# A two-request encoder layer on one core: a lead between the two streams of each merged stage

## The chip, the cores and the metric

The kernel runs on one core of a Trainium2 chip. The metric is device time in microseconds (us) for one launch, in which both request groups pass through the whole layer. Three runs of the kernel before gave 2291.81, 2293.14 and 2294.97 us; the median is 2293.14.

The engines are called as the profile calls them: PE is the matrix engine (PEld its weight loads), ACT the scalar engine, DVE the vector engine, POOL the general one, and SP the engine that issues most of the DMA transfers. Each takes its instructions in a fixed order: an instruction that waits holds back all behind it on the same engine.

## What is computed

One layer is applied to two sequences that share the weights: the prompt (stream 0, 1024 tokens) and the sample (stream 1, 512 tokens), each with 16 meta tokens in front. Cut to what matters:

```
n = rms_norm(h, g_mix);  qa,ka,va,qb,kb,vb = split(n @ w_in)
A: 8 query heads on 2 key heads, softmax(q k^T / 8) v     (q, k normalised and rotated)
B: 4 heads, (softmax(q0 k0^T/8) - lam * softmax(q1 k1^T/8)) v, then a norm
h = h + concat(A, B) @ w_out
n = rms_norm(h, g_ffn)
h = h + (gelu(conv3(n @ w_gate)) * (n @ w_up)) @ w_down        (ConvGLU, 22 column tiles of 128)
out = rms_norm(h, g_final)
```

## The kernel before

Every dense product is done as three passes in a reduced float format (`mm3`, lines 129 to 131: high part by high part, high by low, low by high), so activations and weights are split into a high part (a cast on ACT, line 123) and a low part (a subtraction on DVE or POOL, line 124). `dense` makes one output tile of 128 features by up to 512 tokens from 8 k-tiles, which is 24 matmuls.

For each stream there are four pieces, written as Python generators that yield an estimate of the matmul columns they have just issued:

- `projection`: w_in. Its keys tile comes first; the head norm of a tile is a matmul too (line 232), and waits for squares from ACT and POOL. Queries and keys go to DRAM (`qk`, line 247).
- `attention`: loads q and k with line 370 on SP, makes scores into the PSUM tile `ps_s` (lines 401 and 402), scales them on DVE (line 405), exponentiates on ACT (408), transposes on PE (422), splits into `pt_hi` and `pt_lo`, and multiplies by v into `ps_o` (432 to 437, 446; for heads B line 541 adds the norm). Results go to DRAM (`oT`, lines 482 and 563), and the reciprocals of heads A make a round trip through DRAM (`rT`, lines 458 and 474).
- `mixer_out`: reads `oT` back into `h` (line 612, SP), splits it into `xhi` and `xlo`, multiplies by w_out and adds the input.
- `conv_glu`: the feed-forward part, in 11 groups of two column tiles.

The program runs these stages: the sample's projection alone; stage 1, the sample's attention merged with the prompt's projection; stage 2, the prompt's attention merged with the sample's mixer and ConvGLU; the prompt's mixer; the prompt's ConvGLU alone. `ps_s` is one buffer in both merged stages, and `ps_o` is one too.

What sets the order: `merge` takes the next step of whichever generator is behind by its weighted count (`done[0]/wa` against `done[1]/wb`), and so gives the order in which instructions are traced. A planner then fixes each engine's own order. Of what its model of the timeline has ready it takes, by and large, what was traced first, so that an instruction traced later can still come earlier on its engine. `issue_after(x)` tells it that the instructions traced in a block stand behind x on x's engine, and on that engine alone. In the kernel before, `merge` is never given its last argument, so that nothing is held. At the end of stage 2 the program opens six PSUM buffers and merges the prompt's mixer with what is left of the sample's ConvGLU (line 884).

Of the kernel before, what the change touches and what calls it, by code (L numbers as in the profile page):

```python
# [20 lines left out]
P = 128  # L21
D = 1024
KT = D // P
# [103 lines left out]
def mm3(g, ps, whi, wlo, xhi, xlo, start, stop):  # L127
    nc = g.nc
    nc.tensor.matmul(ps, lhsT=whi, rhs=xhi, start=start, stop=False)  # L129
    nc.tensor.matmul(ps, lhsT=whi, rhs=xlo, start=False, stop=False)  # L130
    nc.tensor.matmul(ps, lhsT=wlo, rhs=xhi, start=False, stop=stop)  # L131


def dense(g, ps, w, xhi, xlo, c0, cw, order=range(KT)):

    whi, wlo = w
    for i, k in enumerate(order):
        mm3(g, ps, whi[:, k * P:(k + 1) * P], wlo[:, k * P:(k + 1) * P],
            xhi[k][:, c0:c0 + cw], xlo[k][:, c0:c0 + cw], i == 0, i == KT - 1)


def load_weight(g, src, lo_engine=None, hi_engine=None):
# [206 lines left out]
def attention(ctx, g, s, side):  # L349
    nc, tc = g.nc, g.tc  # L350
# [43 lines left out]
    def softmax(q, k, l):  # L394

        M = q[0].shape[-1]
        p = pp.tile([P, ne], F32, name="p", tag="p")[:M]
        ps = g.psum.wide(M, nch, kw)
        for i in range(nch):
            kc = k[:, i * kw:(i + 1) * kw]  # L400
            nc.tensor.matmul(ps[:, i], lhsT=q[0], rhs=kc, start=True, stop=False)  # L401
            g.mark = nc.tensor.matmul(ps[:, i], lhsT=q[1], rhs=kc, start=False, stop=True).ins  # L402

        nm = sp.tile([P, 1], F32, name="nm", tag="nm")[:M]
        nc.vector.tensor_scalar(out=p.rearrange("p (i w) -> p i w", i=nch), in0=ps, scalar1=-HD ** -0.5, scalar2=3.0e38,  # L405
                                op0=ALU.mult, op1=ALU.min, accum_out=nm)
        p = p[:, :n]
        nc.scalar.activation(p, p, AF.Exp, bias=nm, scale=-1.0, accum_out=l)  # L408
        return p

    def weighted_v(pl, v, diff):

        W = sum(p.shape[0] for p in pl)
        o = g.psum.tile(P, W, "o")
        v, v_tail = v

        def transposed(k0, kw):
            tps = g.psum.tile(kw, W, "t")
            c = 0
            for p in pl:  # L420
                M = p.shape[0]
                nc.tensor.transpose(tps[:, c:c + M], p[:, k0:k0 + kw], g.ident[:M, :M])  # L422
                c += M
            return tps

        for i in range(nf):
            tps = transposed(i * P, P)
            hi = ptp.tile([P, 512], F32R, name="pt_hi", tag="pt_hi")[:, :W]
            lo = ptp.tile([P, 512], F32R, name="pt_lo", tag="pt_lo")[:, :W]
            split(g, hi, lo, tps)  # L430
            if diff:
                nc.tensor.matmul(o, lhsT=v[:, i, 0:P], rhs=hi, start=i == 0, stop=False)  # L432
                nc.tensor.matmul(o, lhsT=v[:, i, P:2 * P], rhs=hi, start=False, stop=False)  # L433
                nc.tensor.matmul(o, lhsT=v[:, i, 0:P], rhs=lo, start=False, stop=False)  # L434
            else:
                nc.tensor.matmul(o, lhsT=v[:, i, :], rhs=hi, start=i == 0, stop=False)  # L436
                nc.tensor.matmul(o, lhsT=v[:, i, :], rhs=lo, start=False, stop=False)  # L437
            yield 5 * W

        tps = transposed(n - 32, 32)  # L440
        parts = ptp.tile([P, 512], F32R, name="pt_hi", tag="pt_hi")[:, :W]
        split(g, parts[0:32], parts[32:64], tps)
        if diff:
            nc.scalar.copy(parts[64:96], tps)
        rows = v_tail.shape[0]
        nc.tensor.matmul(o, lhsT=v_tail, rhs=parts[:rows], start=False, stop=True)
        yield 2 * W
        return o, W

# [35 lines left out]
    for kv in range(2):  # L485
        k = load_k(KA, kv)
        v = load_v(0, P, kv * P)
        for i in range(4):
            h = kv * 4 + i
            for b in range(nblk):  # L490
                q = load_q(QA + 2 * kv, i, NMETA + 512 * b, 512)
# [8 lines left out]
                o, W = yield from weighted_v(pl, v, False)  # L500
# [13 lines left out]
        o, W = yield from weighted_v([p], v, False)  # L514
# [37 lines left out]
    for h in range(4):  # L552
        ks = [load_k(KB + h // 2 * 2, h % 2 * 2 + m) for m in range(2)]
        v = load_v(1 + h, 2 * P, 0)
        rows = g.oT[s][512 + h * P:512 + (h + 1) * P]
        for blk in blocks:
            c0 = blk[0][0]
# [3 lines left out]
            lead = 1 if c0 < NMETA else 0  # L561
# [22 lines left out]
def mixer_out(g, s, st, side, whole, tag):  # L584

    nc, tc = g.nc, g.tc
    C = SEQS[s] + 2
    h, rstd = st.h, st.rstd
    chunks = token_chunks(s)
    cm = max(w for _, w in chunks)  # L590
    with ExitStack() as es:
        mp = pool(es, g, f"fm{s}", 3, side)
        waiting = []

        def finish():
            while waiting:
                c0, cw, acc = waiting.pop(0)
                mean_rsqrt(g, mp, rstd[:, c0:c0 + cw], acc, cw, tag)

        for group in ([chunks] if whole else [[c] for c in chunks]):  # L600
            if whole:
                (xhi, xlo), base = [[x[:, k] for k in range(KT)] for x in st.x], 0
            else:
                xhi = [mp.tile([P, cm], F32R, name="xhi", tag=f"xhi{k}", bufs=2) for k in range(KT)]
                xlo = [mp.tile([P, cm], F32R, name="xlo", tag=f"xlo{k}", bufs=2) for k in range(KT)]
                base = group[0][0]
            acc = mp.tile([P, sum(w for _, w in group)], F32, name="acc", tag="acc", bufs=1 if whole else 2)
            if group[0][0] == 0:

                nc.vector.memset(h[:, :, C - 1:], 0.0)  # L610
                for k in range(KT):
                    nc.sync.dma_start(out=h[:, k, :C - 1], in_=g.oT[s][k * P:(k + 1) * P])
# [139 lines left out]
        yield 4 * cw  # L752


def merge(a, wa, b, wb, g=None):


    done = [0.0, 0.0]
    while True:
        i = 0 if b is None or done[0] / wa <= done[1] / wb else 1  # L760
        try:
            with g.tc.issue_after(g.mark) if g and i and g.mark else nullcontext():
                done[i] += next((a, b)[i])
# [12 lines left out]
PADD = 8  # L776
ML = 2
NRAW, NW = 2, 3
R1, R2, R3 = (1.0, 1.1), (1.0, 1.1), (1.0, 1.0)


@with_exitstack
def trunk_kernel(ctx, tc, g):
    nc = tc.nc
# [80 lines left out]
    with ExitStack() as es0:  # L865
        p0 = projection(es0, g, 0, "left", "mm", "mm")
        with ExitStack() as es1:
            merge(attention(es1, g, 1, "right"), R1[0], p0, R1[1])
        drain(p0)
    g.psum.close()  # L870
    g.psum = Psum(tc, "psb", mm=2)
# [1 line left out]
    with ExitStack() as es1:  # L873
        st1 = state(es1, 1, "right", True)

        def sample():
            yield from mixer_out(g, 1, st1, "right", True, "mm")
            yield from conv_glu(es1, g, 1, st1, "right", 1)
        f1 = sample()
        with ExitStack() as es0:  # L880
            merge(attention(es0, g, 0, "left"), R2[0], f1, R2[1])
        g.psum.relay(s=6)
        st0 = state(ctx, 0, "left", False)
        merge(mixer_out(g, 0, st0, "left", False, "s"), R3[0], f1, R3[1])
        drain(f1)
    xp = pool(ctx, g, "fx0", 1, "right")
    st0.x = [xp.tile([P, KT, SEQS[0] + 2], F32R, name=nm) for nm in ("xhi", "xlo")]
    g.psum.close()
# [66 lines left out]
```

## Time and profile before

The profiled execution took 2291.51 us; its span from the first instruction to the last is 2289.6 us. The busy times below are those of a window's engines; the clock is the mean granted to PE, as a share of full speed.

| stretch (us) | what runs | PE busy | ACT busy | clock |
|---|---|---|---|---|
| 0 to 157.5 | sample's projection | | | |
| 157.5 to 505.4 | stage 1, up to the last projection tile | 325.0 of 347.9 | 185.6 | 0.97 |
| 505.4 to 585.7 | sample's attention alone, then a stop | 39.7 of 80.3 | 37.6 | 0.78, 0.59 |
| 585.7 to 1323.3 | stage 2, up to the last sample tile but two | 730.9 of 737.6 | 442.4 | 1.00 in the main part |
| 1323.3 to 1402.3 | prompt's attention alone | 57.7 of 79.0 | 56.3 | 0.82, 0.81 |
| 1402.3 to 1540 | prompt's mixer | 122.6 of 137.7 | 73.9 | 0.91 |
| 1540 to 2289.6 | prompt's ConvGLU | | | |

How to read it: where PE is busy for the whole of a stretch at clock 1.00, the stretch lasts as long as its matmuls. Where it isn't, something else ends last, and matmuls that run there cost more than their own time.

### The profile page before, as it was taken

To read this page: it belongs to the slowest core of one execution; us is meant where nothing else is said; L and a number is where in the kernel's file an instruction comes from. 1 tells how busy PE (TensorE), PEld (TensorE's weight loads), DVE (VectorE), ACT (ScalarE), POOL (GpSimd) and SP (SyncE) were. 2 spreads that over 40 slices of the span, in tenths; PEclk is the share of its full clock that TensorE was granted. 3 is DMA by queue.
4 is the path that set the end of the run, shared out by engine and by line. 5 is a ranking of instruction groups with operands and counts; after the bars stand their busy time and mean duration, and the time that the engine had idled before them with its cause. 6 is when DMAs were issued, how large, how long until landed. Compare 5 with 4: busy or idle time off the path is not lost.

```text
span 2289.6 us, 32358 instructions
## 1 busy us (share of the span) xinstructions
PE 2143.9 (94%) x12442; PEld 1918.7 (84%) x12442; DVE 1287.9 (56%) x2203; ACT 1039.3 (45%) x1830; POOL 662.4 (29%) x514
## 2 busy tenths in 40 slices
PE   6888999986799999999999977989999999999997
PEld 6887999885788888888898966988888888888886
DVE  6636564454476667677777764764333444433446
ACT  5434555555454445557777785542122211122224
POOL 4862455440132211224343432431110001111004
PEclk9999999997899999999999987999999999999999
DMA  6563444443412332223333303631111111111112
GB/s 201 180 219 118 150 151 132 157 160 102 149 61 74 93 98 75 81 78 104 102 101 99 104 25 127 199 108 56 37 56 47 46 47 46 42 51 56 46 38 74
DMA packets 114259, 222.76 MB, mean 97 GB/s; under 512 B 16312, under 2 KB 67384, under 8 KB 113592
## 3 DMA queue, kind: packets, MB, share of 16 engines
q1 hardware_dynamic: 85304, 115.82, 15.7%
q10 hardware_dynamic: 28800, 104.87, 14.6%
q8 instruction: 98, 1.61, 0.3%
q14 instruction: 57, 0.47, 0.1%
HBM read 172.10 MB, written 48.55 MB: 96 GB/s over the span
## 4 chain that ended last, share of the span: by engine, by line
PE 66%; DVE 5%; ACT 3%; DMA 2%; issue 1%; POOL 1%; SPq 0%; DVEq 0%; ACTq 0%
PE ps_mm L129 17%; PE ps_mm L130 17%; PE ps_mm L131 17%; PE ps_t L422 4%; PE ps_s L401 3%; PE ps_s L402 2%; PE ps_o L437 1%; PE ps_o L436 1%; DVE p L405 1%; PE ps_o L432 1%; PE ps_o L434 1%; DVE y L729 1%; PE ps_o L433 1%; DVE w_lo L124 1%; DMA w_f<-w_out 1%
## 5 line engine op out<-in xcount | busy, mean ns | idle before, releaser
L129 PE MATMUL ps_mm<-xhi,w_hi 128*128 128x512 f32 (+6 forms) x1968 | 664.7, 338 | 26.2 <-ACT xhi L123 25.5
L130 PE MATMUL ps_mm<-xlo,w_hi 128*128 128x512 f32 (+6 forms) x1968 | 658.8, 335 | 0.0
L131 PE MATMUL ps_mm<-xhi,w_lo 128*128 128x512 f32 (+6 forms) x1968 | 658.8, 335 | 0.0
L129 PEld LDWEIGHTS ps_mm<-xhi,w_hi 128*128 128x128 f32 x1968 | 373.5, 190 | 52.6 <-ACT xhi L123 26.1
L130 PEld LDWEIGHTS ps_mm<-xlo,w_hi 128*128 128x128 f32 x1968 | 373.1, 190 | 25.1 <-issue 0.5
L131 PEld LDWEIGHTS ps_mm<-xhi,w_lo 128*128 128x128 f32 x1968 | 373.1, 190 | 24.7 <-issue 0.6
L123 ACT CAST w_hi<-w_f 128x1024 fp32r<-128x1024 f32 x134 | 139.3, 1048 | 399.2 <-PE ps_mm L130 361.8
L405 DVE TENSOR_SCALAR_CACHE_REDUCE p<-ps_s 114x1044 f32<-114x1044 f32 (+5 forms) x212 | 223.4, 1054 | 129.9 <-PE ps_s L402 103.1
L124 POOL TENSOR_TENSOR a_lo<-gate,a_hi 128x512 fp32r<-128x512 f32 x66 | 98.9, 1498 | 662.7 <-ACT a_hi L123 656.8
L123 ACT CAST pt_hi<-ps_t 128x512 fp32r<-128x512 f32 (+6 forms) x360 | 170.0, 483 | 208.8 <-PE ps_t L422 189.1
L408 ACT ACTIVATE p<-p,nm 114x1040 f32<-114x1040 f32 (+5 forms) x212 | 215.3, 1015 | 90.7 <-DVE p L405 89.9
L703 DVE TENSOR_TENSOR h<-ps_mm,h 128x512 f32<-128x512 f32 (+1 forms) x288 | 182.5, 645 | 129.4 <-PE ps_mm L131 128.2
L124 DVE TENSOR_TENSOR pt_lo<-ps_t,pt_hi 128x512 fp32r<-128x512 f32 (+4 forms) x312 | 172.2, 563 | 107.0 <-ACT pt_hi L123 105.6
L401 PE MATMUL ps_s<-k,q 128*114 128x348 f32 (+4 forms) x552 | 183.8, 338 | 38.5 <-DVE p L405 21.3
L131 PE MATMUL ps_mm<-a_hi,w_lo 128*128 128x512 f32 (+1 forms) x576 | 215.5, 377 | 0.6 <-DVE w_lo L151 0.6
L130 PE MATMUL ps_mm<-a_lo,w_hi 128*128 128x512 f32 (+1 forms) x576 | 215.6, 377 | 0.0
L129 PE MATMUL ps_mm<-a_hi,w_hi 128*128 128x512 f32 (+1 forms) x576 | 214.2, 384 | 0.0
L422 PE MATMUL ps_t<-ident,p 128*128 128x128 f32 (+7 forms) x1188 | 185.6, 272 | 2.4 <-DVE pt_lo L124 2.4
L402 PE MATMUL ps_s<-k,q 128*114 128x348 f32 (+4 forms) x552 | 176.0, 324 | 6.2 <-DMA q<-qk 6.2
L422 PEld LDWEIGHTS ps_t<-ident,p 128*128 128x128 f32 (+7 forms) x1188 | 143.9, 137 | 32.7 <-issue 8.4
L124 DVE TENSOR_TENSOR w_lo<-w_f,w_hi 128x1024 fp32r<-128x1024 f32 x100 | 122.7, 1236 | 83.4 <-ACT w_hi L123 83.2
L691 DVE TENSOR_TENSOR gate<-ps_mm,gate 128x512 f32<-128x512 f32 x66 | 45.6, 690 | 200.2 <-PE ps_mm L131 197.7
(189 smaller groups left out, 3627.6 us busy)
## 6 DMA issues: line engine op xcount, KB each, us to landing
w_f<-w_gate ACTq DMA_DIRECT2D x44, 512.0 KB
w_f<-w_up ACTq DMA_DIRECT2D x44, 512.0 KB
w_f<-w_down ACTq DMA_DIRECT2D x44, 512.0 KB
w_f<-w_in ACTq DMA_DIRECT2D x36, 512.0 KB
w_f<-w_out ACTq DMA_DIRECT2D x32, 512.0 KB
q<-qk SPq DMA_DIRECT2D x48, 256.0 KB
q<-qk SPq DMA_DIRECT2D x48, 171.0 KB
qk<-hi SPq DMA_DIRECT2D x20, 384.0 KB
```

The source lines that it names most:

```text
L123: nc.scalar.copy(hi, src)
L124: (lo_engine or nc.vector).tensor_tensor(out=lo, in0=src, in1=hi.bitcast(F32), op=ALU.subtract)
L129: nc.tensor.matmul(ps, lhsT=whi, rhs=xhi, start=start, stop=False)
L130: nc.tensor.matmul(ps, lhsT=whi, rhs=xlo, start=False, stop=False)
L131: nc.tensor.matmul(ps, lhsT=wlo, rhs=xhi, start=False, stop=stop)
L401: nc.tensor.matmul(ps[:, i], lhsT=q[0], rhs=kc, start=True, stop=False)
L402: g.mark = nc.tensor.matmul(ps[:, i], lhsT=q[1], rhs=kc, start=False, stop=True).ins
L405: nc.vector.tensor_scalar(out=p.rearrange("p (i w) -> p i w", i=nch), in0=ps, scalar1=-HD ** -0.5, scalar2=3.0e38, op0=ALU.mult, op1=ALU.m ...
L408: nc.scalar.activation(p, p, AF.Exp, bias=nm, scale=-1.0, accum_out=l)
L422: nc.tensor.transpose(tps[:, c:c + M], p[:, k0:k0 + kw], g.ident[:M, :M])
L691: nc.vector.tensor_tensor(out=a, in0=up, in1=a, op=ALU.mult)
L703: nc.vector.tensor_tensor(out=hs, in0=ps, in1=hs, op=ALU.add)
```

## The change

`merge` gets a lead and a hold. The count of the second generator starts at `lead` instead of zero: a negative lead lets the second generator run ahead, a positive one the first. The first `hold` steps of the stream that stays behind are traced inside `issue_after(mark)`, where `mark` is the last matmul that the leading stream had traced when the first of them came: on PE they can't be planned ahead of it. `mark` is now the last matmul of a dense tile, or of a block's product with v; before, it was that of a score tile, and unused. In stage 1 the prompt's projection leads the sample's attention by 19200 columns. In stage 2 the prompt's attention leads the sample's mixer and ConvGLU by 60000, and the weights there are equal instead of 1 to 1.1. What is left of the sample's ConvGLU is then traced whole, before the six PSUM buffers and the prompt's mixer. No arithmetic is added or taken away.

```
-def merge(a, wa, b, wb, g=None):
-    done = [0.0, 0.0]
+def merge(g, a, wa, b, wb, lead, hold):
+    done = [0.0, lead]
+    after, held = None, 0
     while True:
         i = 0 if b is None or done[0] / wa <= done[1] / wb else 1
+        if i == (lead > 0) and held < hold:
+            after, held = after or g.mark, held + 1
+            order = g.tc.issue_after(after)
+        else:
+            order = nullcontext()
         try:
-            with g.tc.issue_after(g.mark) if g and i and g.mark else nullcontext():
+            with order:
                 done[i] += next((a, b)[i])
...
-            merge(attention(es1, g, 1, "right"), R1[0], p0, R1[1])
+            merge(g, attention(es1, g, 1, "right"), R1[0], p0, R1[1], LEAD1, HOLD)
...
-R1, R2, R3 = (1.0, 1.1), (1.0, 1.1), (1.0, 1.0)
+R1, R2 = (1.0, 1.1), (1.0, 1.0)
+LEAD1, LEAD2, HOLD = -50 * 384, 60000.0, 4
...
-            merge(attention(es0, g, 0, "left"), R2[0], f1, R2[1])
+            merge(g, attention(es0, g, 0, "left"), R2[0], f1, R2[1], LEAD2, HOLD)
+        drain(f1)
         g.psum.relay(s=6)
         st0 = state(ctx, 0, "left", False)
-        merge(mixer_out(g, 0, st0, "left", False, "s"), R3[0], f1, R3[1])
-        drain(f1)
+        drain(mixer_out(g, 0, st0, "left", False, "s"))
```

Three places show what this does to the engines' orders. In the rows below a name ends in the number of its buffer, which differs between the two programs.

The start of stage 1 on PE. Before, behind the prompt's first projection tile (`ps_mm` from `xhi` is a projection tile, `acc` gives the token norms, `ps_s` is a score tile of the sample):

```order
L208 MATMUL ps_mm_1824<-acc_1742,ones_d_98 128x384
L401 MATMUL ps_s_1704<-k_1692,q_1698 128x264
L208 MATMUL ps_mm_1833<-acc_1742,ones_d_98 128x272
L402 MATMUL ps_s_1704<-k_1692,q_1700 128x264
L401 MATMUL ps_s_1704<-k_1692,q_1698 128x264
```

and after:

```order
L208 MATMUL ps_mm_1783<-acc_1701,ones_d_98 128x384
L208 MATMUL ps_mm_1792<-acc_1701,ones_d_98 128x272
L232 MATMUL ps_mm_1822<-sq_1815,ones_hd_102 128x384
L129 MATMUL ps_mm_1837<-xhi0_1674,w_hi_1694 128x384
...
L401 MATMUL ps_s_1919<-k_1907,q_1913 128x264
```

The first scores have moved behind the head norm of the first tile (L232) and all 24 matmuls of the second. At the other end of the stage, 195 rows of attention stood on PE between the last projection tile and the first row that waits for the sample's `h`; now some 240 do, and 34 fewer stand ahead of the last projection tile.

The start of stage 2, first on PE. Before, at the first tile of the sample's mixer (`ps_mm` from `xhi_6040`; the others are the first block of the prompt's heads A):

```order
L436 MATMUL ps_o_6238<-pt_hi_6416,v_6068 128x512
L422 MATMUL ps_t_6422<-ident_93,p_6077 128x128
L422 MATMUL ps_t_6422<-ident_93,p_6168 128x128
L422 MATMUL ps_t_6422<-ident_93,p_6179 128x128
L422 MATMUL ps_t_6422<-ident_93,p_6220 128x128
L129 MATMUL ps_mm_6141<-xhi_6040,w_hi_6135 128x258
L437 MATMUL ps_o_6238<-pt_lo_6417,v_6068 128x512
```

and after, at the end of the same block and, behind the mark, 82 rows later (the end of the second block):

```order
L436 MATMUL ps_o_6128<-pt_hi_6211,v_6068 128x512
L401 MATMUL ps_s_6502<-k_6065,q_6392 128x348
L402 MATMUL ps_s_6502<-k_6065,q_6394 128x348
...
L437 MATMUL ps_o_6128<-pt_lo_6212,v_6068 128x512
L455 MATMUL ps_t_6283<-ident_93,r_a_6281 4x128
L446 MATMUL ps_o_6128<-pt_hi_6222,v_tail_6070 128x512
...
L402 MATMUL ps_s_6832<-k_6065,q_6772 128x348
L446 MATMUL ps_o_6288<-pt_hi_6382,v_tail_6070 128x512
L129 MATMUL ps_mm_6463<-xhi_6040,w_hi_6457 128x258
```

PE's first mixer tile has moved behind the second block of the prompt's attention. On ACT, at the same place, the casts that feed that tile stood like this before:

```order
L408 ACTIVATE p_6822,l_a_6821<-p_6822,nm_6830 128x1040
L123 CAST pt_hi_6314<-ps_t_6309 128x512
L123 CAST pt_hi_6357<-ps_t_6352 128x512
L123 CAST pt_hi_6368<-ps_t_6363 128x512
L123 CAST pt_hi_6416<-ps_t_6411 128x512
L123 CAST xhi_6040<-h_6042 128x258
```

and stand like this after:

```order
L408 ACTIVATE p_6399,l_a_6398<-p_6399,nm_6407 128x1040
L123 CAST pt_hi_6189<-ps_t_6184 128x512
L123 CAST pt_hi_6200<-ps_t_6195 128x512
L123 CAST pt_hi_6211<-ps_t_6206 128x512
L123 CAST xhi_6040<-h_6042 128x258
L123 CAST xhi_6040<-h_6042 128x256
L123 CAST pt_hi_6222<-ps_t_6217 32x512
```

They have moved by one cast: before, 7 full casts of the first block stood ahead of them, and now 8, with 9 exponentials ahead of them in both. DVE's `xlo` follows them in the same way. On SP the reads of `oT` into `h` (L612) still come last behind a read that waits for `rT` (L474), the read of q (one part before, two now) and the last store of `oT`.

The end of stage 2 on PE. Before, around the last but four of the norms of heads B (L541):

```order
L541 MATMUL ps_o_13742<-o_sq_13740,ones_v_100 128x342
L422 MATMUL ps_t_14021<-ident_93,p_13762 128x114
L422 MATMUL ps_t_14021<-ident_93,p_13827 128x114
L422 MATMUL ps_t_14021<-ident_93,p_13885 128x114
L401 MATMUL ps_s_14476<-k_14127,q_14428 114x348
L402 MATMUL ps_s_14476<-k_14127,q_14430 114x348
```

and after, around the last but two (`ps_mm` from `a_hi` is a tile of the sample's last ConvGLU group):

```order
L541 MATMUL ps_o_13899<-o_sq_13897,ones_v_100 128x342
L422 MATMUL ps_t_14139<-ident_93,p_13919 128x114
L422 MATMUL ps_t_14139<-ident_93,p_13984 128x114
L422 MATMUL ps_t_14139<-ident_93,p_14014 128x114
L129 MATMUL ps_mm_15124<-a_hi_15022,w_hi_15090 128x256
L130 MATMUL ps_mm_15124<-a_lo_15023,w_hi_15090 128x256
```

Before, 283 rows of attention stood behind the last sample tile of the merged part; now 70 do, and the others have sample tiles between them. From there on the prompt's mixer has nearly the same order on PE in both, with the last two small sample tiles near its beginning in both.

More of the change, by code (lines that the diff above doesn't have):

```diff
@@ L130, in mm3 @@
     nc.tensor.matmul(ps, lhsT=whi, rhs=xlo, start=False, stop=False)
-    nc.tensor.matmul(ps, lhsT=wlo, rhs=xhi, start=False, stop=stop)
+    return nc.tensor.matmul(ps, lhsT=wlo, rhs=xhi, start=False, stop=stop).ins
 def dense(g, ps, w, xhi, xlo, c0, cw, order=range(KT)):
@@ L137, in dense @@
     for i, k in enumerate(order):
-        mm3(g, ps, whi[:, k * P:(k + 1) * P], wlo[:, k * P:(k + 1) * P],
-            xhi[k][:, c0:c0 + cw], xlo[k][:, c0:c0 + cw], i == 0, i == KT - 1)
+        g.mark = mm3(g, ps, whi[:, k * P:(k + 1) * P], wlo[:, k * P:(k + 1) * P],
+                     xhi[k][:, c0:c0 + cw], xlo[k][:, c0:c0 + cw], i == 0, i == KT - 1)
 def load_weight(g, src, lo_engine=None, hi_engine=None):
@@ L401, in softmax @@
             nc.tensor.matmul(ps[:, i], lhsT=q[0], rhs=kc, start=True, stop=False)
-            g.mark = nc.tensor.matmul(ps[:, i], lhsT=q[1], rhs=kc, start=False, stop=True).ins
+            nc.tensor.matmul(ps[:, i], lhsT=q[1], rhs=kc, start=False, stop=True)
         nm = sp.tile([P, 1], F32, name="nm", tag="nm")[:M]
@@ L445, in weighted_v @@
         rows = v_tail.shape[0]
-        nc.tensor.matmul(o, lhsT=v_tail, rhs=parts[:rows], start=False, stop=True)
+        g.mark = nc.tensor.matmul(o, lhsT=v_tail, rhs=parts[:rows], start=False, stop=True).ins
         yield 2 * W
```

## Prediction

> **What bounds the kernel now.** I read the page first, then the stages by windows, then who waits for whom, and last the timeline where a window showed PE idle.
>
> ```profile
> span 2289.6 us, 32358 instructions
> PE 2143.9 (94%) x12442; PEld 1918.7 (84%) x12442; DVE 1287.9 (56%) x2203; ACT 1039.3 (45%) x1830; POOL 662.4 (29%) x514
> PE   6888999986799999999999977989999999999997
> PEclk9999999997899999999999987999999999999999
> ```
>
> PE is busy 94% of the span; the next engine has 56%. So the kernel is as long as PE's matmuls plus what PE loses, and PE loses where the slices show less than 9: at the start, in slices 9 to 11, and in slices 23 to 26, where its clock falls too. The change adds no matmul, so only these losses can move. The windows give them (us; PE busy comes first, and clock, DMA share and GB/s last):
>
> ```profile
> 157.50:505.40 347.90, 325.02 (x2072) 304.33 (x2071) 188.11 (x417) 185.59 (x405) 154.82 (x110) 0.97 0.45 144
> 505.40:560.50 55.10, 39.71 (x199) 31.69 (x197) 32.16 (x72) 37.10 (x79) 9.71 (x10) 0.78 0.43 127
> 560.50:585.70 25.20, 0.00 (x0) 0.00 (x0) 0.01 (x1) 0.45 (x2) 0.00 (x0) 0.59 0.46 149
> 585.70:660.00 74.30, 73.01 (x540) 68.20 (x540) 46.07 (x87) 38.13 (x79) 19.15 (x19) 0.98 0.36 110
> 690.00:1300.00 610.00, 608.61 (x3683) 537.76 (x3684) 434.15 (x711) 366.39 (x605) 182.82 (x151) 1.00 0.30 93
> 1323.30:1380.20 56.90, 41.16 (x209) 34.32 (x208) 31.98 (x65) 45.66 (x79) 18.18 (x14) 0.82 0.06 22
> 1380.20:1402.30 22.10, 16.52 (x80) 12.72 (x79) 8.37 (x18) 10.68 (x25) 0.00 (x0) 0.81 0.44 160
> ```
>
> Where both streams run (690 to 1300) PE is busy 608.6 of 610 us at full clock. Where attention is alone (505 to 560, and 1323 to 1402) it is busy for 71 to 75%, with the clock at 0.78 to 0.82. Between them, at 560.5, everything stops for 25 us. The prompt's mixer and ConvGLU behind 1402 keep their order, and I leave them out.
>
> **The end of stage 2, the large term.** These are PE's groups from 1323.3 to 1380.2 (count | busy us, mean ns | idle before), and what matmuls cost when packed at full clock:
>
> ```profile
> L401 PE MATMUL ps_s<-k,q 128*114 128x348 f32 x36 | 13.1, 366 | 9.3 <-DVE p L405 9.1
> L422 PE MATMUL ps_t<-ident,p 114*128 114x114 f32 (+1 forms) x69 | 12.2, 291 | 2.4 <-DVE pt_lo L124 2.4
> L402 PE MATMUL ps_s<-k,q 128*114 128x348 f32 x36 | 12.0, 336 | 0.0
> L432 PE MATMUL ps_o<-pt_hi,v 128*128 128x342 f32 x20 | 8.4, 422 | 1.9 <-DVE o_rs L115 1.7
> L434 PE MATMUL ps_o<-pt_lo,v 128*128 128x342 f32 x20 | 8.4, 420 | 0.0
> L433 PE MATMUL ps_o<-pt_hi,v 128*128 128x342 f32 x20 | 7.9, 394 | 0.0
> L541 PE MATMUL ps_o<-o_sq,ones_v 128*128 128x342 f32 x6 | 3.0, 591 | 1.8 <-ACT o_sq L539 1.8
> 1319.10 0.32 PE L432 MATMUL ps_o<-pt_hi,v 128*128 128x342 f32 x1
> 1319.26 0.32 PE L433 MATMUL ps_o<-pt_hi,v 128*128 128x342 f32 x1
> 1320.28 0.46 PE L422 MATMUL ps_t<-ident,p 114*128 114x114 f32 x3
> 1320.50 0.39 PE L401 MATMUL ps_s<-k,q 128*114 128x348 f32 x1
> ```
>
> Packed, a product with v follows the last after 0.16 us, and three transposes take 0.22, 0.075 each. A score has nearly the same columns (348), so 0.16 too. The stretch therefore holds 72 x 0.16 + 69 x 0.075 + 62 x 0.16 us (the 62 with the two small tail products) and 6 of L541 at about 0.3: 11.5 + 5.2 + 9.9 + 1.8 = 28.4 us of work, done in 56.9. It loses 28.5 us: 15.7 idle (56.9 less 41.2 busy), the rest the slow clock. The one `ps_s` buffer makes each score wait for DVE's read of the last.
>
> In the new order, sample tiles stand between these rows down to the last 70, which are nearly the rows of 1380.2 to 1402.3 (80 matmuls), so those 22 us stay. What stands between is the kind of mix that ran at 99.8% from 690 to 1300, with less attention in it per matmul; ACT, 80% busy here with attention alone, has less to do per us. I leave 2.5 us lost there: **26 us gained**. Bounds: 0, if the attention chain is what ends last all the same, and 28.5.
>
> [...]
>
> ```profile
> 1353.80 0.63 PE L401 MATMUL ps_s<-k,q 128*114 128x348 f32 x1 [2.08 <-DVE p L405]
> 1354.23 0.49 PE L402 MATMUL ps_s<-k,q 128*114 128x348 f32 x1
> 1354.52 0.49 PE L401 MATMUL ps_s<-k,q 128*114 128x348 f32 x1
> ```
>
> Behind a gap of 2.08 us scores follow each other after 0.29 us instead of 0.16. [...]
>
> **The stop at 560, which I expect to stay.** The row of ACT, of PE, and of the queue of SP:
>
> ```profile
> 585.25 1.33 ACT L123 CAST xhi<-h 128x258 fp32r<-128x258 f32 x4 [26.06 <-DMA h<-oT]
> 585.71 0.58 PE L129 MATMUL ps_mm<-xhi,w_hi 128*128 128x258 f32 x1 [25.24 <-ACT xhi L123]
> 555.02 0.54 DVE L544 SCALAR_TENSOR_TENSOR o_b<-o_b,gsub,o_rs 128x306 f32<-128x306 f32 x1
> 565.60 1.99 SPq L563 DMA_DIRECT2D oT<-o_b  x1
> 567.69 0.91 SPq L458 DMA_DIRECT2D rT<-r_rows  x1
> 576.69 0.49 SPq L474 DMA_DIRECT2D o_rb<-rT  x1
> 577.89 0.43 SPq L563 DMA_DIRECT2D oT<-o_b  x1
> 578.38 6.85 SPq L612 DMA_DIRECT2D h<-oT  x8
> ```
>
> PE's wait looks as if moving the mixer tile back would end it. But ACT itself waits 26.06 us, with the casts of `xhi` at its head, and in the new order they stand one cast later. Behind them stand the tail cast of the prompt's first block and all later exponentials; PE's L446 of that block needs that cast. So PE gets a dozen rows further and stops too. The hold works on PE only: DVE's `xlo`, the 8 reads of `h` and the first reads of the residual are as late as before.
>
> When the stop ends is set by SP. The last `o_b` was ready at 555.6, its store went out at 577.9: SP was 22 us behind, with the reads of q, k and halo ahead, and then 9.0 us from the store of `rT` to its read. In the new order PE has 34 attention rows fewer ahead of the last projection tile and some 45 more between it and the stop. Packed, a row costs 39.71 x 0.78 / 199 = 0.156 us; alone, 55.1 / 199 = 0.277. So the last tile comes 34 x 0.156 = 5.3 us earlier, attention ends 45 x 0.277 = 12.5 later from there: +7 us, which SP's 22 us of backlog cover. If they do, the stop ends where it ended, and the extra rows are done in time that was lost anyway: 0. Bounds: -8, if SP gets through its reads earlier with its stores ready; +7 by the sum just made; and +12, if the reads of q for the last blocks are late once more, as here:
>
> ```profile
> 513.23 0.52 PE L401 MATMUL ps_s<-k,q 128*102 128x264 f32 x1 [5.58 <-DMA q<-qk]
> ```
>
> I take **+1 us**, near SP's side.
>
> **The start of stage 2.** PE now does two blocks of heads A there before the first mixer tile, 91 rows more than before behind the point where it stopped: 91 x 0.156 = 14.2 us of work, without sample tiles, while ACT has 16 casts of `xhi` to do and DVE as many `xlo`. At the density of attention alone (28.4 / 56.9 = 0.50) they would take 28 us, so 14 us lost; at that of 585.7 to 660 (73.0 of 74.3 busy) nothing. I take the middle, **+6 us**, since heads A have fewer passes on ACT per matmul than heads B. Later these 91 rows are missing from the mix, but PE is full there.
>
> **The start of stage 1.**
>
> ```profile
> 171.57 0.56 PE L401 MATMUL ps_s<-k,q 128*128 128x264 f32 x1 [8.35 <-DMA q<-qk]
> 179.19 1.65 PE L232 MATMUL ps_mm<-sq,ones_hd 128*128 128x384 f32 x2 [1.98 <-POOL sq L228]
> 177.58 0.49 ACT L286 ACTIVATE sq<-ps_mm 128x384 f32<-128x384 f32 x1 [9.88 <-DMA qk<-y]
> ```
>
> The lead puts the second projection tile ahead of the score that waited 8.35 us for q. But the head norm L232 now stands ahead of both, and its squares wait on ACT until 177.58 for a DMA of the sample's projection, which nothing here moves. So PE waits to 179.2 as before, and the 8 score matmuls which it did in between come later: 8 x 0.156 = **+1 us**. Behind L232 wait the 24 matmuls of the tile and all scores; the first softmaxes are some 10 us later, which matters only through the end of the stage, counted above. Bounds -4 (the tile's 24 matmuls fit in the gap, if the DMA lands earlier) and +4.
>
> **Sum.** -26 + 1 + 6 + 1 = -18 us. The profiled execution took 2291.5 us, so 2273.5 on its scale; the median of the runs shown is 1.6 us above it, so **2275 us**.
>
> **Rivals.**
>
> *The stop goes.* What the change says it does would need PE to have work at 560 that doesn't pass ACT. If SP's chain comes up to 20 us earlier, because its reads of q are spread differently, the sum is -38: 2255 us. For it: SP, not the attention, is last at 577.9. Against it: the 9.0 us of `rT` and the 6.85 us of reads are still in the chain. Chance 0.12.
>
> *Attention still ends last.* Its chain through DVE, ACT and POOL, not PE, sets the end of stage 2, and the sample tiles only fill its gaps. Half the 26 us is then gained: 2288 us. For it: 80% busy on ACT. Against it: the 690 to 1300 window. Chance 0.16.
>
> *Slower: the sample's attention comes too late.* All the scores of its last two blocks are now behind the last projection tile, and their reads of q stand on SP behind 1 MB of k and v and the last stores. If each block waits for its q as at 513.23, and the stores of `oT` wait in turn, the first cast of `xhi` comes 30 us later: 2275 + 29 = 2304 us. It decides from a first cast at about 604 us, 19 us after 585.25, where it eats the other terms. Chance 0.06.
>
> **How the numbers follow.** The forecast, 2275 with its own range of 2265 to 2284, has 0.66. The range for 8 in 10 goes from 2257, halfway into the first rival, to 2290, beyond the second: the unknown terms reach -8 to +12 at the stop and -6 to +8 at the start of stage 2. About 0.2%, 4.6 us, is what a measurement of this kernel can tell from no change. Faster by more than that: the forecast, the first rival and a little over a third of the second, 0.84. Within it: the rest of the second, 0.10. Slower: 0.06.
>
> **What would show it.** The stretch of attention alone at the end of stage 2 shrinks from 79 us to about 22, with PE's clock near 1.00 up to there. ACT's first cast of `xhi` in stage 2 still waits over 20 us for `h`, and starts within 8 us of 585. PE's first mixer tile starts some 20 us after that cast. L232 still starts at about 179 in stage 1. The forecast is wrong if that cast moves by more than 10 us, or if PE is busy for less than 95% in the 35 us ahead of the last sample tile.

## The result and the profile after

The changed kernel takes **2270.51 us** (median of 4 runs, 2269.06 to 2271.93), against 2292.47 us before: a ratio of 0.9902, with a 95% interval of 0.9885 to 0.992. The predicted 2275 us was 4.5 us too high; the profiled execution took 2271.76 us. First the lines of its page that answer to those shown of before:

```profile
span 2270.0 us, 32333 instructions
PE 2139.6 (94%) x12442; PEld 1919.7 (85%) x12442; DVE 1272.2 (56%) x2203; ACT 1039.8 (46%) x1830; POOL 669.2 (29%) x514
PE   7887999986699999999999997999999999999997
PEclk8998999996899999999999998999999999999999
```

Of the thin slices at 23 to 26 one is left; those at 9 to 11 are still there, and a little deeper. The windows of the changed kernel, cut at its own events (us; PE's busy time comes first, the clock, the DMA share and GB/s last):

```profile
503.80:581.20 77.40, 52.59 (x250) 42.30 (x249) 39.95 (x90) 46.38 (x102) 11.91 (x14) 0.74 0.38 113
581.20:596.10 14.90, 0.05 (x2) 0.01 (x1) 1.47 (x5) 1.98 (x6) 0.00 (x0) 0.63 0.66 183
596.10:616.90 20.80, 17.69 (x84) 12.81 (x84) 16.47 (x36) 15.96 (x35) 1.39 (x1) 0.85 0.24 74
616.90:660.00 43.10, 43.10 (x336) 41.24 (x336) 22.87 (x41) 19.96 (x35) 10.59 (x10) 1.00 0.37 104
660.00:690.00 30.00, 30.00 (x226) 28.64 (x224) 18.75 (x32) 14.48 (x28) 9.79 (x11) 1.00 0.31 89
1340.00:1363.30 23.30, 21.92 (x160) 20.64 (x159) 17.83 (x36) 15.37 (x27) 6.55 (x5) 1.00 0.16 54
1363.30:1382.50 19.20, 13.41 (x74) 9.50 (x72) 7.83 (x17) 10.29 (x24) 0.00 (x0) 0.95 0.45 164
```

Attention alone at the end of stage 2 lasts 19.2 us instead of 79.0, and up to it the clock is 1.00. Against that, the sample's attention alone lasts 77.4 us instead of 55.1, and a stop follows as before. The rows at which it begins and ends, from the timeline of the changed kernel:

```profile
584.01 0.43 SPq L563 DMA_DIRECT2D oT<-o_b  x1
584.49 9.57 SPq L612 DMA_DIRECT2D h<-oT  x8
594.12 0.71 ACT L123 CAST xhi<-h 128x258 fp32r<-128x258 f32 x2 [15.52 <-DMA h<-oT]
594.55 0.76 DVE L124 TENSOR_TENSOR xlo<-h,xhi 128x258 fp32r<-128x258 f32 x2 [14.34 <-ACT xhi L123]
596.09 0.79 PE L446 MATMUL ps_o<-pt_hi,v_tail 64*128 64x512 f32 x1 [14.85 <-DVE pt_hi L124]
616.86 0.39 PE L129 MATMUL ps_mm<-xhi,w_hi 128*128 128x258 f32 x1
1382.51 0.66 PE L129 MATMUL ps_s<-xhi,w_hi 128*128 128x344 f32 x1 [1.52 <-ACT xhi L123]
```

PE now stops at L446, a row of the prompt's attention, instead of at the mixer tile: ACT and DVE stand with `xhi` and `xlo` at the head, waiting for `h`.

These events give the account, against 585.25 (first cast), 585.71 (first mixer tile) and 1402.31 us (the prompt's first mixer tile) before:

| | predicted, us | measured, us | from |
|---|---|---|---|
| first cast of `xhi` | +1 | +8.9 | 594.12 - 585.25 |
| from there to the first mixer tile, less 14.2 us of work done ahead of it | +6 | +8.1 | (616.86 - 594.12) - 0.46 - 14.2 |
| from there to the prompt's mixer, plus the same 14.2 us | -26 | -36.7 | 765.65 - 816.6 + 14.2 |
| all, up to the prompt's first mixer tile | -19 | -19.8 | 1382.51 - 1402.31 |

The predicted column leaves out the +1 us of the start of stage 1, which in the measured one is part of the first cast. So two terms were missed by 8 and 11 us, in opposite directions: that the sum came within 2 us of the measured change is in part luck. The split between the second and the third row rests on the prediction's own price of 14.2 us for the work ahead of the tile; their sum does not.

### The profile page after: what moved, and what is told of

Its sections match the earlier page's. It is cut to its first block, busy times and chain, and to the rows that moved or that the text cites. A ratio compares the mean times of both kernels' runs of the same rounds, so it can differ in the third digit from the quotient of the medians.

```text
span 2270.0 us, 32333 instructions
## 1 busy us (share of the span) xinstructions
PE 2139.6 (94%) x12442; PEld 1919.7 (85%) x12442; DVE 1272.2 (56%) x2203; ACT 1039.8 (46%) x1830; POOL 669.2 (29%) x514
## 4 chain that ended last, share of the span: by engine, by line
PE 81%; DMA 6%; DVE 5%; ACT 3%; issue 2%; POOL 1%; SPq 1%; DVEq 0%; ACTq 0%; POOLq 0%
PE ps_mm L129 20%; PE ps_mm L130 20%; PE ps_mm L131 20%; PE ps_t L422 5%; PE ps_s L401 3%; PE ps_s L402 3%; PE ps_o L437 2%; PE ps_o L436 1%; DMA q<-qk 1%; DMA v<-v 1%; PE ps_p L129 1%; PE ps_p L131 1%; PE ps_p L130 1%; PE ps_o L432 1%; DMA w_f<-w_out 1%
## 5 line engine op out<-in xcount | busy, mean ns | idle before, releaser
L532 POOL TENSOR_TENSOR p<-p 114x1040 f32<-114x1040 f32 (+2 forms) x56 | 115.0, 2053 | 128.9 <-ACT p L531 127.0
```

The costliest lines, as they stand in the source:

```text
L532: nc.gpsimd.tensor_tensor(out=p0, in0=p0, in1=p1, op=ALU.add)
```

## The experiments

Each was compared with the kernel before on its own chip. The ratios, with their intervals:

| run | what differs | median, us | ratio to before |
|---|---|---|---|
| e1_second | stage 2's part alone | 2268.69 | 0.9896 [0.9883, 0.991] |
| e2_first | stage 1's part alone | 2299.26 | 1.0034 [1.0021, 1.0046] |
| e3_nohold | no hold | 2268.33 | 0.9894 [0.9881, 0.9908] |
| e4_drain | sample's rest merged with the prompt's mixer | 2325.0 | 1.0142 [1.0128, 1.0155] |
| e5_holdall | hold on PE, ACT and DVE | 2247.35 | 0.9807 [0.9794, 0.9821] |
| e6_both | e5, stage 1 as before | 2251.5 | 0.9824 [0.9811, 0.9838] |
| e7_lead90 | e5, lead 90000 | 2265.31 | 0.9877 [0.9863, 0.989] |
| e9_rows2 | e6, two `r_rows` buffers | 2249.47 | 0.9817 [0.9803, 0.983] |
| e10_poolq | e5, `o_rb` read on POOL's queue | 2246.71 | 0.9807 [0.9793, 0.982] |
| e11_r105 | e5, ratio 1.05 | 2257.28 | 0.985 [0.9837, 0.9864] |
| e12_pool | e9, `o_rb` read on POOL's queue | 2248.54 | 0.9813 [0.9799, 0.9826] |
| e13_poolrows | e10, two `r_rows` buffers | 2247.56 | 0.9805 [0.9792, 0.9818] |

### Which stage's part does what

e1_second undoes the first stage's lead and hold:

```diff
-            merge(g, attention(es1, g, 1, "right"), R1[0], p0, R1[1], LEAD1, HOLD)
+            merge(g, attention(es1, g, 1, "right"), R1[0], p0, R1[1], 0.0, 0)
```

> Only the second merged stage is changed; the first has no lead and no hold, as in the kernel before. Theory A (the gain is all in the second stage; the first stage's lead only delays the end of the sample's attention, and with it the stop): the first cast of xhi from h comes back from 594.1 to 584 to 588 us, the stretch from PE's first mixer tile to the prompt's first mixer tile stays at 766 us within 3, and the time is 2262 us (2259 to 2266). Rival B (the later cast comes from the second stage's own attention rows and reads, which are now ahead of it): the cast stays at 591 to 596 us and the time is 2269 to 2274.

e2_first undoes all of the second stage's part:

```diff
-            merge(g, attention(es0, g, 0, "left"), R2[0], f1, R2[1], LEAD2, HOLD)
-        drain(f1)
+            merge(g, attention(es0, g, 0, "left"), R2[0], f1, 1.1, 0.0, 0)
         g.psum.relay(s=6)
         st0 = state(ctx, 0, "left", False)
-        drain(mixer_out(g, 0, st0, "left", False, "s"))
+        merge(g, mixer_out(g, 0, st0, "left", False, "s"), 1.0, f1, 1.0, 0.0, 0)
+        drain(f1)
```

> Only the first merged stage is changed (lead of the projection and hold); the second stage and the order of the sample's last tiles are as in the kernel before. Theory A: nothing is gained, and the first cast of xhi comes some 9 us later: 2298 us (2294 to 2302). Rival B: the cast stays where it was before (583 to 588 us), and the time is 2289 to 2293.

Alone, the first stage's lead makes the kernel slower by 0.34%, as theory A said (2298 expected, 2299 measured). Alone, the second stage's part gives as much as both together, so the first stage's lead and hold add nothing to it. The waits of PE for reads of q in the sample's attention alone (in all, times, longest) show what the first stage's lead does. In e2_first, from 500 to 575 us:

```profile
PE ps_s L401 <- DMA q<-qk: 14.3, 3, 5.0
PE ps_s L402 <- DMA q<-qk: 3.0, 3, 1.1
```

and in e1_second over the same stretch:

```profile
PE ps_s L401 <- DMA q<-qk: 5.7, 1, 5.7
PE ps_s L402 <- DMA q<-qk: 3.0, 2, 2.7
```

Before, these were 8.2 us (from 500 to 560); in the changed kernel, from 500 to 581.2, they are 16.2:

```profile
PE ps_s L401 <- DMA q<-qk: 13.3, 3, 5.0
PE ps_s L402 <- DMA q<-qk: 2.9, 3, 1.1
```

So the 8 us more come with the first stage's lead and go with it. In e1_second theory A was nearly right on the cast (588.77, against 584 to 588) and wrong on the time: 2268.69 instead of 2259 to 2266. Up to the stop PE runs the same matmuls in the same order there as in the kernel before, and yet the last of the sample's norms of heads B (L541) starts 3.6 us later (553.55 against 549.98), so a single place near 560 us seems good to some 4 us only. The cast is 5.4 us earlier than in the changed kernel, but PE reaches its first mixer tile at 614.56, against 616.86: the time saved is spent in a longer stop (25.9 us at L436 instead of 14.85 at L446).

```profile
588.77 1.33 ACT L123 CAST xhi<-h 128x258 fp32r<-128x258 f32 x4 [26.01 <-DMA h<-oT]
614.56 0.39 PE L129 MATMUL ps_mm<-xhi,w_hi 128*128 128x258 f32 x1
```

### What the hold is for

e3_nohold sets the number of held steps to 0 and keeps both leads:

```diff
-LEAD1, LEAD2, HOLD = -50 * 384, 60000.0, 4
+LEAD1, LEAD2, HOLD = -50 * 384, 60000.0, 0
```

> The changed kernel with its leads but without any hold: PE's order is the scheduler's alone. Its first mixer tile stands 90 rows earlier on PE, and 91 attention rows instead of 70 stand behind the last sample tile. Theory A (a hold on PE alone buys little: ACT and DVE are blocked by the casts of xhi and by xlo either way, so PE merely stops at the tile instead of at L446): a wait of 12 to 25 us of PE's mixer tile for xhi instead of the 14.85 us at L446, and 2273 us (2268 to 2278). Rival B (PE's hold carries the gain of the second stage): 2282 us or more.

The hold on PE alone buys nothing: 0.9894 without it, 0.9902 with it, and the intervals overlap. As theory A said, PE now waits at the tile itself. The wait is longer than at L446 and longer than A's 12 to 25 us, but the tile starts 21 us earlier (595.72 against 616.86), with some 90 attention rows fewer ahead of it:

```profile
595.72 0.89 PE L129 MATMUL ps_mm<-xhi,w_hi 128*128 128x258 f32 x2 [28.46 <-ACT xhi L123]
```

e5_holdall holds the same four steps on ACT and DVE too. `g.marks` has the last matmul, the last cast and the last subtraction of the block:

```diff
-        split(g, parts[0:32], parts[32:64], tps)
+        act = nc.scalar.copy(parts[0:32], tps).ins
+        dve = nc.vector.tensor_tensor(out=parts[32:64], in0=tps, in1=parts[0:32].bitcast(F32), op=ALU.subtract).ins
...
+        g.marks = [g.mark, act, dve]
...
-            after, held = after or g.mark, held + 1
-            order = g.tc.issue_after(after)
+            after, held = after or (g.marks if lead > 0 else [g.mark]), held + 1
+            for m in after:
+                order.enter_context(g.tc.issue_after(m))
```

> As the changed kernel, but in the second stage the hold also applies on ACT and DVE: the sample's first four steps stand behind the last tail cast and the last tail subtraction of the prompt's attention on these engines too. Theory A (the stop exists since the casts of xhi and the xlo stand in ACT's and DVE's queues ahead of the prompt's softmax): PE's idle of 14.9 us shrinks to under 6 us in all, and the time is 2259 us (2255 to 2263). Rival C (SP is the engine that stops all: behind the read of rT the reads of q for the prompt's blocks wait too): PE stops for another 12 to 17 us nearby, and the time is 2268 to 2273.

The one long stop goes, and another 1% of the time: 2247 us, better than theory A's 2259. The first cast of `xhi` no longer waits for anything, and from 545 us up to its first mixer tile PE's longest wait is 3.53 us:

```profile
575.67 1.12 PE L422 MATMUL ps_t<-ident,p 128*128 128x128 f32 x4 [3.53 <-ACT r_rows L459]
588.89 1.33 ACT L123 CAST xhi<-h 128x258 fp32r<-128x258 f32 x4
602.42 0.58 PE L129 MATMUL ps_mm<-xhi,w_hi 128*128 128x258 f32 x1 [2.10 <-ACT w_hi L123]
1361.74 0.66 PE L129 MATMUL ps_s<-xhi,w_hi 128*128 128x344 f32 x1 [1.52 <-ACT xhi L123]
```

The first mixer tile is 14.4 us earlier than in the changed kernel (602.42 against 616.86). The other 6.3 us up to 1361.74 are gained behind it; in this order 27 attention rows instead of 70 stand behind the last sample tile. Theory A's "under 6 us in all" did not come true: from 545 us to its first mixer tile PE is still idle for 14.9 us, in many short waits, against 23.4 us in the changed kernel.

e6_both puts e1_second's edit on top of e5_holdall.

> The first stage as in the kernel before, and the hold of the second stage on PE, ACT and DVE. If both theories A hold, the two gains add: 2251 us (2246 to 2256). If the earlier end of the sample's attention and the hold save the same idle time, 2259 to 2263.

The 2251.5 us lie in the range for two gains that add, but only because e5_holdall alone had already gained more than was expected of it. The two don't add: 0.9824 against 0.9807, the intervals overlap. With the hold on three engines the first stage's lead is neither good nor bad by these runs.

### The end of stage 2

e4_drain goes back to merging what is left of the sample with the prompt's mixer; the lead, the ratio and the hold are kept:

```diff
-        drain(f1)
         g.psum.relay(s=6)
         st0 = state(ctx, 0, "left", False)
-        drain(mixer_out(g, 0, st0, "left", False, "s"))
+        merge(g, mixer_out(g, 0, st0, "left", False, "s"), 1.0, f1, 1.0, 0.0, 0)
+        drain(f1)
```

> The changed kernel, but what is left of the sample when the prompt's attention has been traced is again merged with the prompt's mixer, as in the kernel before. 394 attention rows instead of 70 then stand on PE with no sample tile between them, and sample tiles stand among the mixer's. Theory A (the gain at the end of the second stage comes from tracing the sample whole): the alone rows cost 324 x (0.277 - 0.136) = 46 us, and the mixer, which loses some 26 us, gives back 10 to 20: 2301 us (2292 to 2310). Rival B (lead and ratio carry the gain, the mixer takes back all the rest): 2265 to 2280.

It is slower than the kernel before, by 1.4%, and slower than A's range. From the end of the last sample tile to the prompt's mixer the attention rows run alone for 115.3 us:

```profile
1246.40:1361.70 115.30, 80.05 (x401) 66.07 (x399) 66.84 (x116) 82.84 (x147) 28.63 (x21) 0.85 0.18 60
```

That is 96.1 us more than the 19.2 of the changed kernel for 324 rows, 0.30 us each instead of the 0.277 that I used. Less 0.136 each in the mix (the prediction's 28.4 us for 209 rows) this is an estimate of 52 us lost, and the time is 54.5 us longer than the changed kernel's median: the mixer gives back nothing that shows. So the gain of the end hangs on tracing the sample whole; the lead and the ratio without it lose. Tracing it whole without lead and ratio was not run.

### How far to lead

e7_lead90 sets `LEAD2` of e5_holdall to 90000, and e11_r105 its ratio `R2` to (1.0, 1.05).

> As e5_holdall, with a lead of 90000 instead of 60000: one more block of the prompt's attention (72 rows on PE) ahead of the first mixer tile. Theory A (the lead of 60000 already covers SP's delay: the casts of xhi no longer waited): the 72 rows run alone at 0.277 instead of 0.156 us a row, 9 us more, of which some fills idle time: 2253 us (2249 to 2260). Rival B (PE still loses time to the late h and more work ahead of it fills that): 2238 to 2244.

> As e5_holdall, with the ratio of the second stage at 1.05 instead of 1.0: the first mixer tile stands 78 rows earlier on PE, and 41 instead of 27 attention rows are behind the last sample tile. Theory A (rows alone ahead of the tile are what is still lost): 78 x (0.277 - 0.156) = 9 us less ahead of it and 2 us more at the end: 2240 us (2236 to 2244). Rival B (h isn't there yet, ACT and DVE block again with the casts of xhi at their heads, and PE stops): 2250 to 2260.

Both are worse than e5_holdall, and from opposite sides. With more lead (2265 us, worse than A's range of 2249 to 2260) the first mixer tile of the profiled execution comes at 617.15 instead of 602.42: the 72 rows more ahead of it cost 14.7 us, 0.20 each, and filled little that was idle. With ratio 1.05 the tile stands 78 rows earlier, `h` isn't there, and the stop is back, as rival B said:

```profile
587.68 0.41 ACT L123 CAST xhi<-h 128x258 fp32r<-128x258 f32 x1 [17.22 <-DMA h<-oT]
591.69 0.66 PE L401 MATMUL ps_s<-k,q 128*128 128x348 f32 x1 [18.40 <-DVE res L627]
```

### What is left of the stop

In e6_both ACT waited 13.67 us for the store of `r_rows` to land before it could write the next. e9_rows2 gives the prompt's attention two such buffers:

```diff
-        rows = sp.tile([P, P], F32, name="r_rows", tag="r_rows", bufs=1)[:4]
+        rows = sp.tile([P, P], F32, name="r_rows", tag="r_rows", bufs=2 - s)[:4]
```

> As e6_both, with two buffers instead of one for the r_rows of the prompt's attention. In e6_both the copy into r_rows on ACT waited 13.67 us for the store of the last one to land, and PE 12.65 us behind it. Theory A (that one buffer is what is left of the stop): PE's wait for r_rows near 573 falls under 3 us and the time is 2241 us (2237 to 2246). Rival B (SP, which stands behind that store's landing with its next reads, brings another wait of the same length): 2248 to 2253.

e10_poolq (on e5_holdall) and e12_pool (on e9_rows2) take the read that waits for `rT` off SP's queue:

```diff
-            nc.sync.dma_start(out=rb, in_=r.broadcast_to([HD, oa.shape[1]]))
+            (nc.gpsimd if s == 0 else nc.sync).dma_start(out=rb, in_=r.broadcast_to([HD, oa.shape[1]]))
```

> As e5_holdall, but the reads of o_rb from rT of the prompt's attention are issued by POOL instead of SP, so that SP no longer stands 9 us behind the landing of rT with the last store of oT, the reads of h and the next q. Theory A (SP's chain still sets the start of the sample's mixer): the reads of h go out some 9 us earlier (568 instead of 577.6) and the time is 2240 us (2235 to 2244). Rival B (with the hold on ACT and DVE the casts of xhi, which waited for nothing in e5_holdall, come when the attention ahead of them is done; an earlier h is of no use): 2246 to 2250.

> As e9_rows2 (first stage as in the kernel before, hold on three engines, two r_rows buffers), with the reads of o_rb on POOL. In e9_rows2 SP waited 9.6 us for rT, the casts of xhi 8.47 us for h, and PE 11.71 us behind them. Theory A (the wait for rT in SP's queue is what is left of the stop): these waits go, and the time is 2240 us (2235 to 2245). Rival B (SP's queue holds the reads of h back for other reasons, or they land no earlier): 2247 to 2252.

e13_poolrows is e10_poolq with e9_rows2's edit.

> As e10_poolq, with two r_rows buffers for the prompt's attention. In e10_poolq PE still waited 7.03 us for the r_rows copy, which waited for the store of the last one. Theory A (this wait is lost time): it goes, and the time is 2240 us (2236 to 2244). Rival B (the stretch is limited by attention alone, not by any one wait in it: a wait that goes comes back elsewhere): 2245 to 2250.

Rival B's time came out in all four, and its mechanism in e9_rows2 and e10_poolq. In e9_rows2 the wait of ACT for the store of `r_rows` is gone (its copy at 561.31 waits 0.37 us, and for PE), and PE waits as long as before, a block later, behind casts of `xhi` that wait for `h`:

```profile
586.62 0.41 ACT L123 CAST xhi<-h 128x258 fp32r<-128x258 f32 x1 [8.47 <-DMA h<-oT]
592.61 1.12 PE L422 MATMUL ps_t<-ident,p 128*128 128x128 f32 x4 [11.71 <-ACT r_rows L459]
```

In e10_poolq the reads of `h` go out at 570.24 instead of 577.63, and PE's first mixer tile comes at 597.81 instead of 602.42, but the time is the same:

```profile
570.24 11.49 SPq L614 DMA_DIRECT2D h<-oT  x8
574.60 1.12 PE L422 MATMUL ps_t<-ident,p 128*128 128x128 f32 x4 [7.03 <-ACT r_rows L459]
587.81 0.71 ACT L123 CAST xhi<-h 128x258 fp32r<-128x258 f32 x2
597.81 0.58 PE L129 MATMUL ps_mm<-xhi,w_hi 128*128 128x258 f32 x1
```

In e13_poolrows PE's wait for `r_rows` falls from 7.03 to 2.5 us, but a short wait for `w_hi` (2.7 us) that e10_poolq did not have comes instead, and the first mixer tile is no earlier (600.20). In e12_pool the mechanism was theory A's: the reads of `h` go out at 571.94 instead of 576.64, the cast waits for 2.90 us instead of 8.47 and PE for 5.2 instead of 11.71. Yet the time does not show it.

```profile
583.37 0.41 ACT L123 CAST xhi<-h 128x258 fp32r<-128x258 f32 x1 [2.90 <-DMA h<-oT]
```

Six versions with the hold on three engines, a lead of 60000 and equal weights lie between 2246.7 and 2251.5 us. Which of their waits is removed makes no difference that these runs can tell. Two of them, e6_both and e9_rows2, still have one wait of PE of 12.65 and 11.71 us, so it is not the absence of one long wait that pays. All six have the first mixer tile at 597.8 to 602.4 instead of 616.86, and 27 rows behind the last sample tile instead of 70. What limits the stretch from 545 to 602 us then, in which PE is busy for 36 to 45 of 57.4 us in the six, stays open: attention alone is the best candidate, but no run tested it by itself.

## Why the prediction was right, step by step

**What bounds the kernel: right.** PE's instructions are the same 12442 and its busy time is nearly the same, 2139.6 us instead of 2143.9, in a span of 2270.0 instead of 2289.6: what moved was mostly its losses.

**The end of stage 2: right in mechanism, the largest term, sized at -26 and measured at -36.7.** The sample tiles filled the gaps, and the attention chain did not end last: in the 35 us ahead of the last sample tile PE was busy for 96%.

```profile
1328.30:1363.30 35.00, 33.62 (x219) 30.75 (x218) 24.88 (x47) 24.25 (x39) 12.34 (x9) 1.00 0.17 57
```

The size failed at two places. I left 2.5 us lost in the mix and took the 22 us behind it as unchanged; by the windows 59.8 us less are spent alone (79.0 less 19.2), and the 213 rows that were there are 29 us of work in the mix at 28.4 / 209 = 0.136 each, an estimate: 31 us gained. The other 6 us fit a window that I did not quote, between 660 and 690 us of the kernel before:

```profile
660.00:690.00 30.00, 27.09 (x152) 23.92 (x153) 25.51 (x46) 20.35 (x44) 12.17 (x17) 0.83 0.13 44
```

152 matmuls in 30 us, against 226 in the changed kernel's row for the same stretch: 2.9 us idle, and, by an estimate from the clock of 0.83, 27.09 x 0.17 = 4.6 us of slower work. At its beginning (660 to 667) some blocks of the prompt's heads A ran almost alone, while in the changed kernel PE waits for nothing from its first mixer tile to 690. My bound of 28.5 us for the term was the loss of one window, not of all that the change could fill. One reading in it was off too: I put the whole 12.8 us between 41.16 busy and 28.4 of work to the clock, but at a mean clock of 0.82 the clock's share is, by estimate, 41.16 x 0.18 = 7.4 us. The rest seems to be how busy time is counted: a row lasts 0.32 us where the next follows after 0.16, so a row with nothing close behind it counts for more.

**The stop: right that it stays, and why; its end was sized at +1, measured at +8.9**, inside the bounds of -8 to +12 but beyond the 8 us that I gave as the mark. ACT's wait for `h` and DVE's behind it are there as described, though ACT's is 15.52 us and not the "over 20" that I named as a sign. e5_holdall shows the claim that the hold works on PE only: with the hold on ACT and DVE as well that stop goes (from 545 us to the first mixer tile PE's longest wait is 3.53 us instead of 14.85).

The attention ended much later than I had summed: its last `o_b` was ready at 574.20 instead of 555.56, 18.6 us and not 7, with PE's waits for q at 16.2 instead of 8.2 us as in the upper bound. But SP's backlog did cover that: SP stored it 9.8 us later still. The step that failed is the next one, that SP would then reach its last store when it did before. Of SP's queue this is a row before:

```profile
550.83 6.13 SPq L370 DMA_DIRECT2D halo<-qk  x8
```

and these, with one row of DVE, are from after:

```profile
550.60 9.47 SPq L370 DMA_DIRECT2D halo<-qk  x6
573.67 0.53 DVE L544 SCALAR_TENSOR_TENSOR o_b<-o_b,gsub,o_rs 128x306 f32<-128x306 f32 x1
573.95 0.45 SPq L458 DMA_DIRECT2D rT<-r_rows  x1
```

SP begins the last reads of `halo` at the same time and stores `rT` 6.3 us later (573.95 against 567.69). Its last store of `oT` follows at 584.01 instead of 577.89, and the reads of `h` then take 9.57 us instead of 6.85: 6.1 + 2.7 = 8.8 of the 8.9 us. e3_nohold agrees that SP and not the attention sets this: there the last of the sample's norms of heads B (L541) starts at 554.87 on PE, 11.9 us earlier than in the changed kernel (566.74), and the first cast comes at 595.26 all the same, behind a wait of 28.54 us for `h`. Why SP's own reads took longer is not shown. The later cast seems to go with the first stage's lead, since it comes at 594.12, 596.42 and 595.26 in the changed kernel, e2 and e3, which have the lead and no hold on ACT and DVE (e4 has too, and its cast is not shown), and at 585.25 and 588.77 without the lead (before, e1). But e5_holdall has the lead too, and SP's last store goes out at 577.15 there.

**The start of stage 2: +6 predicted, +8.1 measured.** PE was busy for 17.69 of the 20.8 us from 596.1 on, at a clock of 0.85, denser than attention alone and thinner than the mix, as assumed. Some 1.5 of the 8.1 us lie between the cast and PE's restart at L446 (1.97 us instead of 0.46), which I had left out. The first mixer tile came 22.7 us behind the cast ("some 20").

**The start of stage 1: right.** L232 starts at 178.70, behind a wait that is now 13.03 us instead of 1.98:

```profile
178.70 1.65 PE L232 MATMUL ps_mm<-sq,ones_hd 128*128 128x384 f32 x2 [13.03 <-POOL sq L228]
```

The order "projection first" buys nothing there, since what comes first still waits for a DMA: ACT's L286 waited for it for 10.02 us, until 177.10.

**The rivals.** The stop did not go. Attention did not end last. The slower case, a later sample attention, did happen by half: the first cast moved 8.9 us, not the 19 at which it decides. e2_first is that case without the gain to pay for it, and it is slower.

## What to carry to other kernels

When one engine holds its place for work that isn't ready, look at the queues of all engines. Here a hold on the engine that waits last, PE, only moved its wait, from the mixer tile to L446 (2268.3 us without the hold, 2270.5 with it), and the hold paid when it was put on the engines that stand in between, ACT and DVE (2247.4 us). The head start of one stream over the other could be wrong on both sides here: with less of it (ratio 1.05) the follower's inputs weren't there and the time was 2257.3 us, with more (lead 90000) the leader ran alone for longer and the time was 2265.3. And when a change spreads thin work over dense work, price every window in which the thin work runs alone, the short ones included.

## What was not expected of the hardware

The granted clock did not go by the length of one gap in these two profiles. In the kernel before it fell from 1.00 to 0.50 behind waits of at most 1.11 us, at the end of a few thin microseconds. A wait of 2.24 us followed at 665.01, and from 667 to 670, when PE was busy all the time, the clock was still 0.50 (windows of 3 us, and the row behind the wait of 1.11 us):

```profile
655.00:658.00 3.00, 2.42 (x13) 1.49 (x12) 2.98 (x6) 2.15 (x7) 0.00 (x0) 1.00 0.54 171
658.00:661.00 3.00, 1.89 (x9) 1.29 (x8) 2.96 (x6) 2.36 (x5) 0.00 (x0) 0.90 0.10 28
661.00:664.00 3.00, 1.77 (x7) 1.36 (x5) 3.00 (x4) 1.24 (x4) 2.13 (x2) 0.50 0.26 102
667.00:670.00 3.00, 3.00 (x17) 2.92 (x15) 2.17 (x4) 1.39 (x3) 0.95 (x2) 0.50 0.02 6
660.42 0.66 PE L401 MATMUL ps_s<-k,q 128*128 128x348 f32 x1 [1.11 <-DVE p L405]
```

In the changed kernel the clock was 1.00 from 1371 to 1374 in spite of a wait of 1.70 us up to 1371.5: the products with v behind it follow each other after 0.16 us.

```profile
1371.50 0.42 PE L432 MATMUL ps_o<-pt_hi,v 128*128 128x342 f32 x1 [1.70 <-DVE o_rs L115]
1371.76 0.32 PE L433 MATMUL ps_o<-pt_hi,v 128*128 128x342 f32 x1
1371.92 0.32 PE L434 MATMUL ps_o<-pt_lo,v 128*128 128x342 f32 x1
```

And in e5_holdall the same small store and the read that waits for it lay 9.0 us apart one time and 3.5 us the next. SP issued nothing in between for the first pair, behind reads of `halo`, k and q. For the second it issued two reads of q and a store in between, so that only 1.0 of the 3.5 us passed between the end of that store's issue (593.01) and the read.

```profile
566.35 0.54 SPq L460 DMA_DIRECT2D rT<-r_rows  x1
575.34 0.49 SPq L476 DMA_DIRECT2D o_rb<-rT  x1
590.53 0.27 SPq L460 DMA_DIRECT2D rT<-r_rows  x1
594.03 0.49 SPq L476 DMA_DIRECT2D o_rb<-rT  x1
```
